# Two orders changed in a 4096 x 4096 matmul: quarter sums of A behind a sum of B, and the two units of one B block swapped

## The chip, the cores and the metric

The kernel runs on one core of a Trainium2 chip. The metric is the device time of one execution in microseconds (us). Before the change three runs gave 1533.63, 1534.99 and 1537.55 us, so the median is 1534.99 us.

## The reference

```python
def reference(a, b, alpha):            # a, b: 4096 x 4096 float32, alpha = 0.01
    x = np.matmul(a, b)
    return np.where(x > 0, x, alpha * x)
```

## The kernel before

**Tiling.** The output is cut into 4 row groups g and 4 column groups j of 1024 each; one pair (g, j) is a region. The first region, (0, 0), is computed plainly while the inputs arrive. The other fifteen follow in the order of the list `regions`: (0,1) (0,2) (0,3), then (1,2) (1,0) (1,3) (1,1), then (2,2) (2,0) (2,3) (2,1), then (3,2) (3,0) (3,1) (3,3). Within a region A is four blocks of 512 x 2048 (a11, a12, a21, a22) and B four blocks of 2048 x 512 (b11, b12, b21, b22), held in float16. Each block is two units of depth 1024, called k = 0 and k = 1; a unit of B is one tile of 128 x 4096 elements.

**Seven products instead of eight.** A region is made by a Winograd scheme: VectorE forms sums of A (s1, s2, s3, s4) and sums of B, TensorE runs seven products, and the results are added in PSUM or in SBUF. `PRODUCTS` (L653) lists the A operand and the place of the B operand of each. Product 0 is a11 by b11. The sums of B overwrite its blocks: at L1052 b12 becomes b12 - b22, at L1055 b11 becomes b11 + (b12 - b22), which product 2 takes (s2 by b11's place), and at L1116 b11's place becomes that sum minus b22, called t1 here, which product 4 takes (s1 by b11's place). A full product is 64 matmuls on each unit k, 128 columns of weights by 512 columns, into four PSUM banks.

**Quarters.** From row group 1 on, unless the next region begins a new row group, products 5 and 6 (the sixth and seventh) are themselves done by the same scheme in quarters: seven products of 16 matmuls with 256 columns. Their A operands are quarter sums of a22 and of s4 (`sums_of_a`, L693): four sums of 128 x 2048 elements, numbered 1 to 4, each stored to DRAM by SyncE (SP) as it is made (`kept_q`, L702), because every later region of the group loads them back (`load_sums`). Their B operands are quarter sums of b21 and b22 (`t3_of_b`, `sums_of_b`). In every region after the first of a group (g > 0) product 3 (the fourth) is done so too. `keep_x21` stores one more quarter of the block itself.

**Rooms.** `x_pool` has three rooms that are reused in turn. In the first region of a group they hold s2, s1 and s4; the next tile asked for, `t` at L1106, four quarters long, gets the room of s2 and can be written only when product 2 has read s2. `a16_pool` has three rooms of one quarter each; a room is free again when the store of what it held has landed. The eight DMA semaphores of SP and ScalarE are used in turn, so each issue also waits for the one eight before it.

**Order of work.** The schedule is written out by hand: each engine works through its instructions in program order. In a first region VectorE has, between products 1 and 4: the adds of product 1 (L973), the leaky step (L313), two sums for b21 (L1090), `keep_x21` and the four quarter sums of s4 (L1096, L1097), t1 in two sums (L1116, one for each k), the four quarter sums of a22 (L1121), then the quarter sums of b21 (L1161, L1162), the difference of b22 (L1163), `add_v` (L1164) and the adds of product 4 and of the quarter products (L973, L862). The quarter sums of s4 go to `new_a16`, and so do sums 1 to 3 of a22; the fourth goes to `t[:, 3]`, and the three quarter sums of b21 to `t[:, 0]`, `t[:, 1]`, `t[:, 2]`.

**B's loads.** `fetch_b` asks for the next region's blocks as soon as the products that read them have gone through: b12 behind product 3, b11 behind product 4 (L1184), b21 and b22 behind the quarter products. Most go through GpSimd's queue, half a unit (512 KB) at a time (L533). A second region's b11 is asked for by the first region with k = 0 ahead of k = 1, since `ks` there is (0, 1); in the second region itself `ks` is (1, 0), and product 0 reads k = 1 first:

```python
ks = (1, 0) if in_quarters else (0, 1)
todo = [(k, c) for k in ks for c in range(KC)]
```

The sums of B at L1052 and L1055 follow `ks` too: b12's unit 1, b11's unit 1, b12's unit 0, b11's unit 0, with the memset that releases the load of half of s2 between the first two (L1054).

Of the kernel before, what the change touches and what calls it, by code (L numbers as in the profile page):

```python
# [24 lines left out]
KC = 8  # L25
# [23 lines left out]
def kernel(  # L49
# [153 lines left out]
    def a_cols(t, c, mt, is_plain=False):  # L203
        rows = slice(mt * P, (mt + 1) * P)
        return plain(t)[:, c, rows] if is_plain else t[:, c // 2, rows, c % 2]
# [132 lines left out]
    order = [("b", 0), ("a", 0, 0, 1), ("a", 1, 0, 1), ("a", 2, 0, 1), ("a", 3, 0, 1)]  # L338
# [3 lines left out]
    for what, i, *more in order:  # L342
        if what == "a":
            r, tiles = more
            k = slice(r * rw, (r + 1) * rw)
# [106 lines left out]
    for i in range(1, len(steps)):  # L452
        t, h, u, first, last = steps[i]
# [19 lines left out]
        t, h, u, first, last = steps[i]  # L473
# [108 lines left out]
    def operand(g, name, k):  # L582
        if name[0] == "s":
            return s[g, name, k]
        return at[g, int(name[1]) - 1, 2 * (int(name[2]) - 1) + k]
# [90 lines left out]
    def quarters_of_a(g, name):  # L676
        return {(h, k): operand(g, name, k)[:, :, h * HALF:(h + 1) * HALF, :] for h in range(2) for k in range(2)}
# [15 lines left out]
    def sums_of_a(g, name, room):  # L693

        x = {key: q.rearrange("p c m e -> p c (m e)") for key, q in quarters_of_a(g, name).items()}
        made = {}

        def make(n, x0, x1, op):
            made[n] = room(n)
            f = lambda t: made[t].rearrange("p (c m) -> p c m", m=2 * HALF) if isinstance(t, int) else x[t]  # L700
            nc.vector.tensor_tensor(f(n), f(x0), f(x1), op)
            nc.sync.dma_start(kept_q[name][n - 1], made[n])  # L702

        make(1, (1, 0), (1, 1), ADD)
        make(2, 1, (0, 0), SUB)
        make(3, (0, 0), (1, 0), SUB)
        make(4, (0, 1), 2, SUB)

    def x21(g, name):
        return operand(g, name, 0)[:, :, HALF:, :]  # L710

    def by_chunk(t):
        return t.rearrange("p c m e -> p c (m e)") if len(t.shape) == 4 else t.rearrange("p (c m) -> p c m", m=2 * HALF)

    def keep_x21(g, name):
        if g < G - 1:
            nc.sync.dma_start(by_chunk(kept_x21[name]), by_chunk(x21(g, name)))
# [45 lines left out]
    def new_a16(_=None):  # L763
        return a16_pool.tile([P, QUARTER], DT, name="q16", tag="a16")
# [18 lines left out]
    for i, (g, j) in enumerate(regions):  # L783

        ks = (1, 0) if in_quarters else (0, 1)
# [11 lines left out]

        def product(n, banks, first):
            name, half, nt = PRODUCTS[n]
            todo = [(k, c) for k in ks for c in range(KC)]  # L800
            order = [(mt, k, c) for k, c in todo for mt in range(MT)]
            if n == 0 and late_s2:

                order = [(mt, k, c) for k in ks for mts in ((0, 1), (2, 3)) for c in range(KC) for mt in mts]
            for mt, k, c in order:
                t = operand(g, name, k)
                nc.tensor.matmul(  # L807
                    banks[mt], a_cols(t, c, mt, t is first_a), B(half, nt, k)[:, c, :],
                    start=first and (k, c) == todo[0], stop=(k, c) == todo[-1], skip_group_check=not first,
                )  # L810
# [188 lines left out]
        def fetch_a(h, half, n):  # L999
            if n == 0:  # L1000
                coming["rows", h, half] = small_pool.tile([P, 16], FP32, name="rows", tag=f"rows{half}")
            coming[h, half][n][0]()
# [21 lines left out]
        first_of_group = i == 0 or regions[i - 1][0] != g  # L1024
        in_quarters = g > 0 and not turning
        in_fourth = in_quarters and not first_of_group
        second_of_group = in_fourth and regions[i - 2][0] != g
# [3 lines left out]
        if first_of_group and g:  # L1031
            keep_s2(g)

        product(0, y, True)
        if second_of_group:
            sums_of_s3(g, (2,))
# [5 lines left out]
        if have_t2:  # L1042
            for k in ks:
                t = have_b[i, k, 0] = b_pool.tile([P, KC, NT], DT, name="b", tag="b11")
# [23 lines left out]
        bring_a(0, 0, range(3 if g else 4))  # L1068

        product(1, z, True)  # L1070
        add(u1, z)
        leave(u1_pairs, 0, 0)
# [18 lines left out]
        if turning and g:  # L1091
            t3_of_b(quarters_of_b(i, 0, 1))
            for n in range(3):
                fetch_a(0, 1, n)
        if first_of_group and g:
            keep_x21(g, "s4")  # L1096
            sums_of_a(g, "s4", new_a16)  # L1097
        if not g:
            bring_a(0, 1)

        product(2, y, False)
        if late_ones:
            late_ones[0].begin()
        u2_pairs, u2 = keep(y, 1 - side)
        if g:
            t = x_pool.tile([P, 4, QUARTER], DT, name="q", tag="x")  # L1106
# [10 lines left out]
        if late_ones:  # L1117
            late_ones[0].end()
        if in_quarters and first_of_group:
            sq = {4: t[:, 3]}  # L1120
            sums_of_a(g, "a22", lambda n: sq.setdefault(n, sq[4] if n == 4 else new_a16()))  # L1121
            keep_x21(g, "a22")
# [106 lines left out]
    with tc.If(even == 0):  # L1229
        for m in range(M // RM):  # L1230
            a_blocks = []
            for u in range(KU):
                t = a_pool.tile([P, KC // 2, RM, 2], BF16, name="a", tag=f"a{u // 2 + 1}{m % 2 + 1}")
# [6 lines left out]
            for n in range(N // NT):  # L1240
                banks = [new_bank(n % 2 * 4 + mt) for mt in range(MT)]
                cols = slice(n * NT, (n + 1) * NT)
                for u in range(KU):
                    t = b_pool.tile([P, KC, NT], BF16, name="b", tag=f"b{u // 2 + 1}{n % 2 + 1}")
# [8 lines left out]
                for mt in range(MT):  # L1253
                    t = c_pool.tile([P, 2, NT], FP32, name="c", tag=f"c{side}")[:, 0]
# [44 lines left out]
```

## Time and profile before

| what | value |
|---|---|
| median of three runs | 1534.99 us (1533.63 to 1537.55) |
| the profiled execution's own time | 1536.2 us |
| its span, first to last instruction | 1534.2 us |
| busy: TensorE / VectorE / ScalarE / GpSimd | 1524.3 / 1158.9 / 425.5 / 258.5 us |
| granted TensorE clock | 0.999 |
| HBM read and written, over the span | 300 GB/s |

The span is split by region as follows, by the first matmul of each in the timeline: (1,2) begins at 411.1 us, (1,0) at 505.2, (2,2) at 784.6, (2,0) at 878.1, (3,2) at 1157.6, (3,0) at 1251.7. A full product takes 13.8 us there, a product in quarters 12.2 us. In the table a busy time is the sum over the whole span; where an engine's queue stood still, and for whom, is in the views of waits and in the timeline.

### The profile page before, as it was taken

Reading aid. Unit: us, or ns where it says so; the run is one execution under the profiler, and the core shown is the slowest. Engines: PE = TensorE matmul, PEld = TensorE weight load, DVE = VectorE, ACT = ScalarE, POOL = GpSimd, SP = SyncE. Lnnn points to the kernel's source line nnn. Section 1 sums busy time; section 2 is a strip of 40 time slices with the busy share of each in tenths; the row PEclk is TensorE's granted clock in tenths of the full one; section 3 lists DMA queues with packets and bytes.
Section 4 is the critical chain, followed back from the end, with each engine's and each line's share of the span. In section 5 each row is a group of like instructions: output and inputs, shape, how many; then the busy total and the mean of one; then the engine's idle time right before and its main releaser. Section 6 shows DMA issues by size and latency. Waiting matters only on the chain. (4 is left out here: it accounts for less than half of the span.)

```text
span 1534.2 us, 21785 instructions
## 1 busy us (share of the span) xinstructions
PE 1524.3 (99%) x8667; PEld 847.1 (55%) x8667; DVE 1158.9 (76%) x1207; ACT 425.5 (28%) x730; POOL 258.5 (17%) x426
## 2 busy tenths in 40 slices
PE   9999999999999999999999999999999999999998
PEld 4444444444446567574544747557544475746656
DVE  4368867765699686768769698676976987687677
ACT  2201344646310213103641130312464103041210
POOL 5641110143202011022220001010331100101000
PEclk9999999999999999999999999999999999999999
DMA  9999995998879999899797939669899892948723
GB/s 246 186 215 203 237 281 169 180 197 172 231 277 287 258 278 275 251 289 255 170 288 266 321 148 208 260 157 322 166 241 283 235 349 72 294 162 190 301 97 140
DMA packets 192002, 351.26 MB, mean 229 GB/s; under 512 B 18705, under 2 KB 131601, under 8 KB 178834
## 3 DMA queue, kind: packets, MB, share of 16 engines
q0 software_dynamic: 119808, 112.22, 46.2%
q1 hardware_dynamic: 65458, 211.98, 37.0%
q10 hardware_dynamic: 6624, 25.56, 4.4%
q8 instruction: 70, 1.15, 0.3%
q14 instruction: 42, 0.34, 0.1%
HBM read 344.98 MB, written 114.82 MB: 300 GB/s over the span
## 5 line engine op out<-in xcount | busy, mean ns | idle before, releaser
L807 PE MATMUL ps<-b,a 128*128 128x512 f16 x2624 | 571.1, 379 | 0.5 <-DMA b<-in_b_dram 0.3
L807 PE MATMUL ps<-b,s 128*128 128x512 f16 x2240 | 489.2, 379 | 0.0
L807 PEld LDWEIGHTS <-a 128*128 128x128 f16 x2624 | 256.7, 98 | 308.8 <-issue 1.5
L807 PEld LDWEIGHTS <-s 128*128 128x128 f16 x2240 | 219.1, 98 | 262.5 <-issue 0.4
L589 DVE TENSOR_TENSOR b<-b 128x4096 f16<-128x4096 f16 x104 | 234.6, 2286 | 42.7 <-DMA b<-in_b_dram 34.1
L533 POOL DMA_DIRECT2D b<-in_b_dram x128 | 94.9, 746 | 860.1 <-PE ps L752 437.2
L820 ACT COPY c<-ps 128x512 f32<-128x512 f32 x164 | 84.8, 596 | 469.1 <-PE ps L807 433.3
L142 DVE STREAM_TRANSPOSE a<-a 128x512 uint32<-128x512 uint32 (+2 forms) x120 | 127.0, 1106 | 100.8 <-DMA a<-in_a_dram 100.8
L133 POOL DMA_DIRECT2D a<-in_a_dram x252 | 137.6, 554 | 266.8 <-ACT junk L608 98.2
L608 ACT ACTIVATE junk<-a 128x512 bf16<-128x512 f16 x192 | 121.1, 631 | 99.1 <-DMA a<-in_a_dram 93.8
L752 PEld LDWEIGHTS <-q 128*128 128x128 f16 x1424 | 139.3, 98 | 16.7 <-issue 0.6
L313 DVE SCALAR_TENSOR_TENSOR c<-c 128x1024 f32<-128x1024 f32 (+2 forms) x123 | 141.5, 1190 | 3.8 <-ACT c L820 3.5
L973 DVE TENSOR_TENSOR c<-ps,c 128x512 f32<-128x512 f32 x140 | 87.5, 682 | 55.5 <-PE ps L807 41.8
L231 ACT ACTIVATE sq<-b 128x2048 bf16<-128x2048 f16 x64 | 118.3, 1910 | 37.1 <-DVE sq L240 29.4
L752 PEld LDWEIGHTS <-a 128*128 128x128 f16 x1200 | 117.4, 98 | 18.0 <-issue 0.4
L283 PE MATMUL ps<-b,a 128*128 128x512 f16 x512 | 112.4, 379 | 0.6 <-DVE part L324 0.2
L752 PE MATMUL ps<-b,q 128*128 128x256 f16 x784 | 92.0, 273 | 0.4 <-DVE c L862 0.4
L752 PE MATMUL ps<-b,a 128*128 128x256 f16 x752 | 88.3, 273 | 0.0
L283 PEld LDWEIGHTS <-a 128*128 128x128 f16 x512 | 49.7, 98 | 61.2 <-issue 2.1
L909 ACT COPY c<-ps 128x512 f32<-128x512 f32 x9 | 5.3, 586 | 269.7 <-PE ps L752 148.3
L752 PEld LDWEIGHTS <-s 128*128 128x128 f16 x624 | 61.0, 98 | 7.1
L862 DVE TENSOR_TENSOR c<-ps,c 128x512 f32<-128x512 f32 x80 | 52.2, 683 | 14.4 <-PE ps L752 14.4
(104 smaller groups left out, 904.8 us busy)
## 6 DMA issues: line engine op xcount, KB each, us to landing
b<-in_b_dram POOLq DMA_DIRECT2D x136, 512.0 KB, 11.7
out_dram<-c SPq DMA_DIRECT2D x240, 256.0 KB, 6.3
a<-in_a_dram POOLq DMA_DIRECT2D x244, 128.0 KB, 5.8
b<-kept_half SPq DMA_DIRECT2D x28, 1024.0 KB, 10.9
b<-kept SPq DMA_DIRECT2D x20, 1024.0 KB, 9.2
q<-kept_qs ACTq DMA_DIRECT2D x40, 512.0 KB, 7.8
s<-kept_s SPq DMA_DIRECT2D x18, 1024.0 KB, 7.7
q<-kept_qa SPq DMA_DIRECT2D x28, 512.0 KB, 7.3
```

What stands on the lines that cost most here:

```text
L133: nc.gpsimd.dma_start(a16[32 * q:32 * q + 32], src.rearrange("(g i) w -> i g w", i=32))
L142: nc.vector.transpose(part.rearrange("p c m e -> p c (m e)").bitcast(U32) .rearrange("p c (g i) -> p g c i", i=32), src[:, :, i * n:(i + 1 ...
L231: nc.scalar.activation(to, self.parts[n], SQUARE)
L283: nc.tensor.matmul(ps, a_cols(at[0, h, u], c, mt, (h, u) == (0, 0)), bt[0, u, nt][:, c, :], start=first, stop=last,)
L313: nc.vector.scalar_tensor_tensor(t, t, alpha, t, op0=MULT, op1=MAX if alpha <= 1 else MIN)
L533: nc.gpsimd.dma_start(t[:, c:c + 4, :], b_rows(j, u, c, 4, nt, g > 0))
L589: nc.vector.tensor_tensor(f(to), f(x0), f(x1), op)
L608: nc.scalar.activation(junk, piece[:, q, :], SQUARE, accum_out=to[:, 4 * n + q:4 * n + q + 1])
L752: nc.tensor.matmul(to[m], xq[:, c // 2, rows, c % 2], yq[:, c, :], start=first and c == 0 and m < banks, stop=c == KC - 1, skip_group_chec ...
L807: nc.tensor.matmul(banks[mt], a_cols(t, c, mt, t is first_a), B(half, nt, k)[:, c, :], start=first and (k, c) == todo[0], stop=(k, c) == t ...
L820: nc.scalar.copy(kept[mt], banks[mt])
L973: nc.vector.tensor_add(to, bank, to)
```

## The change

Two edits. In the first region of a group (g > 0), `keep_x21` and the quarter sums of s4 move behind t1, and they are written to `t`, in the room of s2, instead of to `a16_pool`: sum 1 to `t[:, 3]`, sum 2 to `t[:, 0]`, sum 3 to `t[:, 2]`, sum 4 to `t[:, 1]`. In the second region of a group product 0 takes b11's unit 0 first and unit 1 second. The other products, and the sums of B, keep their order.

```diff
         def product(n, banks, first):
             name, half, nt = PRODUCTS[n]
-            todo = [(k, c) for k in ks for c in range(KC)]
+            ks_here = (0, 1) if n == 0 and second_of_group else ks
+            todo = [(k, c) for k in ks_here for c in range(KC)]
             order = [(mt, k, c) for k, c in todo for mt in range(MT)]
             if n == 0 and late_s2:
-                order = [(mt, k, c) for k in ks for mts in ((0, 1), (2, 3)) for c in range(KC) for mt in mts]
+                order = [(mt, k, c) for k in ks_here for mts in ((0, 1), (2, 3)) for c in range(KC) for mt in mts]
...
-        if first_of_group and g:
-            keep_x21(g, "s4")
-            sums_of_a(g, "s4", new_a16)
         if not g:
             bring_a(0, 1)
 
         product(2, y, False)
...
         for k in ks:
             b_sum(B(0, 0, k), B(1, 1, k), B(0, 0, k), SUB)
         if late_ones:
             late_ones[0].end()
         if in_quarters and first_of_group:
+            keep_x21(g, "s4")
+            sums_of_a(g, "s4", lambda n: t[:, {1: 3, 2: 0, 3: 2, 4: 1}[n]])
             sq = {4: t[:, 3]}
             sums_of_a(g, "a22", lambda n: sq.setdefault(n, sq[4] if n == 4 else new_a16()))
             keep_x21(g, "a22")
```

## The prediction

> **What bounds the kernel now.** First the page: its first line says how busy TensorE is, the rest of the span is all that any reordering can give.
>
> ```profile
> PE 1524.3 (99%) x8667; PEld 847.1 (55%) x8667; DVE 1158.9 (76%) x1207; ACT 425.5 (28%) x730; POOL 258.5 (17%) x426
> ```
>
> The span is 1534.2 us, so TensorE idles 9.9 us, start and tail included. A gain over 0.3% (4.6 us, about what a measurement of this kernel can tell from no change) would need half of that. Second, TensorE's waits in the stretch from 411 to 600 us, regions (1,2) and (1,0); columns: us in all, times, longest.
>
> ```profile
> PE ps L752 <- DVE c L862: 0.4, 1, 0.4
> PE ps L807 <- DMA b<-in_b_dram: 0.3, 1, 0.3
> ```
>
> Both lie where the change works. Third, the timeline around them, and around product 2 of (1,0); columns: start, us, engine and operation, in brackets the idle time before and who ended it.
>
> ```profile
> 489.46 0.70 PE L752 MATMUL ps<-b,q 128*128 128x256 f16 x5 [0.45 <-DVE c L862]
> ...
> 505.18 1.89 PE L807 MATMUL ps<-b,a 128*128 128x512 f16 x8
> ...
> 507.38 4.91 PE L807 MATMUL ps<-b,a 128*128 128x512 f16 x22 [0.31 <-DMA b<-in_b_dram]
> ...
> 528.25 2.29 DVE L589 TENSOR_TENSOR b<-b 128x4096 f16<-128x4096 f16 x1 [8.61 <-DMA b<-in_b_dram]
> 530.50 0.06 DVE L770 MEMSET s<- 128x1 f16 x1
> 530.63 2.29 DVE L589 TENSOR_TENSOR b<-b 128x4096 f16<-128x4096 f16 x1
> ...
> 533.27 9.01 PE L807 MATMUL ps<-b,s 128*128 128x512 f16 x41
> ```
>
> See three things. At 489.46 a quarter product was held by VectorE's adds. At 507.38 product 0 of (1,0) was held by a load: b11's unit 1, which it reads first, landed at 507.33, unit 0 had landed at 496.03. And at 533.27 product 2 starts without a wait, but its B operand was finished at 530.63 + 2.29 = 532.92, only 0.35 us earlier, behind b22's unit 1, which landed at 528.13. Matmul starts are 0.216 us apart (0.109 with 256 columns); by starts the first stall costs 0.720 - 0.109 = 0.61 us, the second 0.686 - 0.216 = 0.47 us.
>
> Fourth, VectorE in (1,2):
>
> ```profile
> 458.58 1.21 DVE L701 TENSOR_TENSOR q<-s 128x2048 f16<-128x2048 f16 x1
> 459.82 1.23 DVE L701 TENSOR_TENSOR q<-q,s 128x2048 f16<-128x2048 f16 x1
> 460.97 1.22 DVE L701 TENSOR_TENSOR q<-s 128x2048 f16<-128x2048 f16 x1
> 462.71 1.23 DVE L701 TENSOR_TENSOR q<-s,q 128x2048 f16<-128x2048 f16 x1 [0.52 <-DMA kept_qs<-q]
> 463.85 4.49 DVE L589 TENSOR_TENSOR b<-b 128x4096 f16<-128x4096 f16 x2
> 468.37 1.23 DVE L701 TENSOR_TENSOR q<-a,a 128x2048 f16<-128x2048 f16 x1
> 470.41 1.23 DVE L701 TENSOR_TENSOR q<-q,a 128x2048 f16<-128x2048 f16 x1 [0.81 <-DMA kept_qs<-q]
> 472.40 1.23 DVE L701 TENSOR_TENSOR q<-a 128x2048 f16<-128x2048 f16 x1 [0.76 <-DMA kept_qs<-q]
> ```
>
> Its only idle time between 421 and 500 us is for rooms whose stores have not landed: 2.09 us. The pair at 463.85 is t1: its unit 0 is done about 466.1, product 4 starts at 466.30. Fifth, the DMA engines by stretch (the last two numbers: share of the 16 engines, GB/s):
>
> ```profile
> 459.00:463.00 4.00, 4.00 (x20) 1.83 (x19) 3.44 (x4) 0.00 (x0) 1.49 (x2) 1.00 0.50 144
> 463.00:480.00 17.00, 17.00 (x81) 7.74 (x79) 15.32 (x12) 2.05 (x4) 2.96 (x4) 1.00 1.12 290
> 480.00:505.00 25.00, 24.55 (x225) 21.75 (x224) 21.13 (x25) 1.17 (x2) 5.92 (x8) 1.00 1.14 293
> 505.00:526.00 21.00, 20.69 (x99) 9.40 (x97) 12.66 (x18) 10.54 (x10) 1.48 (x2) 1.00 1.18 258
> 526.00:531.00 5.00, 5.00 (x25) 2.27 (x24) 2.67 (x3) 0.00 (x0) 0.00 (x0) 1.00 1.24 206
> ```
>
> From 463 to 531 they are full without a break; half a unit of b22 issued at 498.65 lands 27 us later. What is added to that backlog, or missed before it, moves b22.
>
> **The change part by part.** Per first region four sums of 1.22 us, four stores of 512 KB and, in groups 1 and 2, one store of a quarter move; nothing is added or removed.
>
> *Region (1,2), VectorE.* t1 starts at 458.58 (product 2 ended at 452.65, so no new wait) and is done at 463.1. The s4 sums follow until 467.8: s2's room is free since product 2. The a22 sums want 467.8, 469.0, 470.1 and 471.3; 1 to 3 find their rooms free now. New waits stand for `t`: the fourth for the store of s4's sum 1, b21's three sums (wanted at about 473.7, 474.9, 476.0) for those of sums 2, 3 and 4. The stores would be issued at 464.4, 465.5, 466.6 and 467.8. Three stores of s4 took 2.8, 7.2 and 8.1 us in the trace, those of a22 6.7 to 7.7 landing 2.0 apart. With 7.5 for the first and 2.0 between them they land at 471.9, 473.9, 475.9 and 477.9: waits of 0.6, 0, about 0.3 and about 0.8 us. VectorE thus has 2.09 - 1.7 = 0.4 us less idle time (ends: 2.8 us stores, 2.1 less; 10.2 us, the slowest a22 store of the third group, some 2 us more). Behind it queue `add_v` and the adds up to the one at 488.73 that TensorE waited for, with no gap from 480.60 on: the 0.61 us stall shrinks by 0.4, taken as 0.5 with the 2.0 spacing at its kinder end (0.61 gone; worst, 2 added).
>
> *Regions (2,2) and (3,2), VectorE.* Idle for stores there is 0.36 and 0.40 us; ahead of product 4's adds it idles 4.38 (853.24) and 1.97 us (1226.77). With a22's latencies of 6.7 to 8.2 us in (2,2) the new waits come to 0.1 us. In (3,2), 5.3 to 10.2 us, the last would be up to 2.2 late against 1.97 plus the 0.40 saved: no time on TensorE.
>
> *The queues.* SP's order stays the same: product 1's stores, the quarter of s4, its sums, a22's. No store of c waits behind them, the next are issued at 487.70. But the s4 stores are moved past GpSimd's first two loads of b12, issued at 459.86 and 460.60. Before, the first store ran while the DMA engines were half idle (share 0.50) and landed at 462.6, as the loads' packets began. Now it is issued at 464.4, into the full stretch: 512 KB more stand in the backlog. Price: stores of 256 KB with the queue to themselves land 0.64 us apart (548.12 to 550.06), so 1.29 us for 512 KB. Ends: 0 if the loads use the idle half, and four stores, 5.2 us, if none is made up. I take 1.3, since what is not full before 463 is full after. Every later landing up to 531 moves by it, b22's unit 1 to 529.4; b11's and b21's have room (b21's unit 0 at 524.8, wanted at 525.0).
>
> *Region (1,0).* Product 0 finds unit 0 there: 0.47 us gone, and unit 1 (507.3 + 1.3) is wanted only 6.9 us after the start. b11's unit 1 is now read until the end of product 0, so the sum at L1055 waits for that; in (1,0) and (2,0) it starts at 530.63 and 903.43, long after products that end at 519 and 892. In (3,0) it moves from 1261.26 to about 1265.5, behind it b12's and b11's unit 0 (4.5 us) and the measuring adds at 1270.22, which start about 1272.3; the adds of product 1 at 1278.85 come 0.2 late at most, and VectorE waits 2.84 us for TensorE at 1293.31. Product 2 at 1279.3 has its operand at 1267.8. Cost 0, hidden by product 1 (13.8 us). The memset and the load of s2 stand ahead of that sum and do not move.
>
> *The sum.* TensorE comes to product 2 of (1,0) 0.5 + 0.47 = 0.97 us earlier, at 532.3. Its operand is finished at 532.92 + 1.3 = 534.2 and it starts at 534.25: 0.98 us later than before. TensorE is full afterwards, so that remains: +1.0 us, span 1535.2, the profiled execution 1537.2. That execution stood 1.2 us above the median; on the median it is 1534.99 + 1.0, and I say 1535.9. Ends: backlog 0 gives 532.97 against 533.27, -0.3; a backlog of 2.0 gives +1.7.
>
> A rule that speaks against the change: GpSimd's two issues at 459.86 and 460.60 would now lie beside t1. In the trace the issue at 466.77 (0.74 us) ran inside t1's second sum (466.05 to 468.34) and took what all sixteen of this stretch take, 740 to 752 ns; the next came 1.43 us later, after that sum had ended. The Trainium skill, "SBUF — State Buffer", section "A bandwidth-pool intuition that's wrong (but worth ruling out)", says that descriptors GpSimd writes for its DMAs can be held until VectorE's operation ends. The first row does not bear it out for this shape, the second might. By that rule the time would be 1539.2 (worked out among the rivals), by the first row it stays 1535.9.
>
> **The rivals.**
> Gain stands: the backlog is made up before 528, and product 2 has its operand by 532.3. For it: loads without stores beside them land faster (838.70 and 842.47 in (2,2), issued at 833.43 and 834.17). Against it: no stretch below a share of 1.1 until 531. The bound is both stalls, -1.1: 1533.9; with the 0.5 us stall near 1171, behind a chain of loads of A, also gone, 1533.4.
>
> Stores hold VectorE in the first regions: at 10.2 us per store 2 us in (1,2), on top of the sum: +1 to +3, 1536 to 1538. For it: 10.2 occurs; against it: only behind four loads.
>
> Slower by over 0.3%: b22's unit 1 comes late by all four s4 stores, 4 x 1.29 = 5.2 us. Product 2 of (1,0) starts at 532.92 + 5.2 = 538.1, +4.9, 1539.9. It decides from a landing of 532.8 instead of 528.13. Against it: three of the four stores already ran in the full stretch.
>
> GpSimd held by t1: the two issues wait from 459.86 until 463.1, 3.2 us in which the engines idle; with the 1.0 above +4.2, 1539.2. Against it the issue at 466.77.
>
> Nothing to see: stalls and backlog as now, 0.
>
> **How the numbers follow.** Forecast 0.6; gain stands 0.2; stores hold VectorE 0.08; four stores late 0.05; GpSimd held 0.03; nothing 0.04. Faster by over 0.3%: 0.01, out of the gain's share, since 4.6 us are not there. Slower by over 0.3%: the 0.05, half of the 0.03, and 0.01 for sums of several, 0.07 rounded down. Within: 0.92. The range reaches from the gain's far end, 1533.4, to the end of held VectorE, 1538.0, and leaves out about 0.1; the forecast's own range is 1534.7 to 1536.7.
>
> **What would show it.** t1 at 458.6 in (1,2), no wait of the sums on rooms before the fourth of a22, the stall at 489.46 under 0.2, product 0 of (1,0) without a wait; b22's unit 1 landing near 529.4 and a wait of about 2 us ahead of product 2 of (1,0), named for VectorE. Wrong if that landing stays at 528.1 or comes after 531, if VectorE waits over 3 us for stores in (1,2), or if (2,0) or (3,0) show a wait at product 2 that is not there now (0.1 us at 905.87).

## The result and the profile after

The kernel before took 1534.96 us (median of 22 runs, 1532.74 to 1537.79), the changed kernel 1542.78 us (median of 22 runs, 1534.14 to 1547.50). The ratio is 1.0041, with a 95% interval of 1.0029 to 1.0054: slower by 0.41%, outside the predicted range of 1533.4 to 1538.0. The changed kernel's runs also spread over 13 us where those of the kernel before spread over 5; a likely reason is given below. Two runs of the experiments, one of e1 at 4187.71 us and one of e4 at 2444.05 us, stand far above the others of their kernels, and the times below leave them out.

The profiled execution of the changed kernel took 1547.45 us, near the upper end, with a span of 1545.5 us, 11.3 more than the span before. The same work is done, as the busy times on the page of the changed kernel show; the second line, a group's (busy and mean ns of one, then the idle time before it and what ended it), names what was waited for:

```profile
PE 1526.6 (99%) x8667; PEld 847.7 (55%) x8667; DVE 1159.6 (75%) x1207; ACT 425.5 (28%) x730; POOL 258.4 (17%) x426
...
L809 PE MATMUL ps<-b,a 128*128 128x512 f16 x2624 | 574.9, 381 | 8.6 <-DMA b<-in_b_dram 8.6
```

TensorE's waits in the changed kernel over the whole run (us in all, times, longest); the two stalls that the prediction listed for before are not among them, and three others are:

```profile
PE ps L809 <- DMA b<-in_b_dram: 8.6, 2, 5.8
PE ps L809 <- DVE b L589: 1.6, 1, 1.6
```

In the timeline of the changed kernel they stand one in each second region, at (1,0), (2,0) and (3,0) (start, us, engine and operation, in brackets the idle time before and its releaser):

```profile
504.70 27.36 PE L809 MATMUL ps<-b,a 128*128 128x512 f16 x126
533.70 2.53 PE L809 MATMUL ps<-b,s 128*128 128x512 f16 x11 [1.64 <-DVE b L589]
...
878.56 8.80 PE L809 MATMUL ps<-b,a 128*128 128x512 f16 x40
893.17 9.06 PE L809 MATMUL ps<-b,a 128*128 128x512 f16 x29 [5.81 <-DMA b<-in_b_dram]
...
1259.67 8.80 PE L809 MATMUL ps<-b,a 128*128 128x512 f16 x40
1271.26 6.04 PE L809 MATMUL ps<-b,a 128*128 128x512 f16 x21 [2.80 <-DMA b<-in_b_dram]
```

Product 0 and product 1 of (1,0) now run through from 504.70 without a wait, and product 2 waits 1.64 us for VectorE, as predicted. The wait that costs most is in product 0 of (2,0), 40 matmuls after its start: 32 on b11's unit 0 and 8 on the first half of its unit 1 (a full product is 64 matmuls in all, 32 on each unit; the section on the kernel before counts 64 on each, which is a slip; product 0 of a second region takes two of its four banks through a whole unit ahead of the other two, so the second half is wanted after 8 matmuls on the first). The load of the second half of unit 1 had not landed. (3,0) repeats it.

Starts of the same matmul in the two profiled executions show where the time went:

| milestone | before, us | after, us | difference |
|---|---|---|---|
| first of (1,2) | 411.05 | 410.75 | -0.30 |
| first of (1,0) | 505.18 | 504.70 | -0.48 |
| product 2 of (1,0) | 533.27 | 533.70 | +0.43 |
| first of (2,0) | 878.14 | 878.56 | +0.42 |
| first of (3,0) | 1251.67 | 1259.67 | +8.00 |
| end of the span | 1534.2 | 1545.5 | +11.3 |

So the part that the prediction summed, up to product 2 of (1,0), came out at +0.43 where it said +0.98 (at +0.73 if the 0.30 by which (1,2) began earlier is taken out). Then 7.6 us are lost between the start of (2,0) and that of (3,0), and 3.3 us after it. By starts of matmuls the three waits are 1.81, 5.97 and 2.96 us. Behind the second 13 matmuls and behind the third 7 started about 0.427 us apart instead of 0.216, which is 2.64 and 1.34 us more. That is 14.7 us; less the two stalls that went (0.61 and 0.47) it would be 13.6, against 11.3 of span. The rest are losses that the kernel before has and the changed one has not: gaps between matmul starts of 0.11 us at 905.6, 0.34 at 1106.9 and 0.60 from 1171.4 to 1172.6, together about 1.0, and a longer tail of the span, 6.80 us from the start of the last matmul against 5.83.

The granted clock falls with those slow matmuls. Windows of the changed kernel around the wait in (2,0) (busy us and instructions of TensorE, its weight loads, VectorE, ScalarE, GpSimd; granted clock; DMA share; GB/s):

```profile
880.00:894.00 14.00, 8.19 (x38) 3.51 (x36) 12.07 (x19) 10.92 (x7) 0.00 (x0) 0.92 1.07 361
894.00:900.00 6.00, 6.00 (x19) 2.27 (x18) 4.78 (x5) 4.50 (x4) 0.00 (x0) 0.62 0.31 120
```

In the six microseconds after the wait TensorE is busy throughout, at a clock of 0.62. The Trainium skill, "TensorE: Matmul & The Clock Gate", Part 1, says that after an idle window of about 3.4 us TensorE's clock is halved and that it takes about as long of work to come back, after a number of matmuls that varies with the phase of a free-running window. The runs agree with the halving and the variation; a wait of 2.96 us was already enough here.

Why that load was late is seen one region earlier. VectorE in (1,2) of the changed kernel, where the prediction expected waits for rooms:

```profile
453.34 8.90 DVE L589 TENSOR_TENSOR b<-b 128x4096 f16<-128x4096 f16 x4
462.14 1.23 DVE L701 TENSOR_TENSOR q<-s 128x2048 f16<-128x2048 f16 x1
463.41 1.23 DVE L701 TENSOR_TENSOR q<-q,s 128x2048 f16<-128x2048 f16 x1
...
470.35 1.22 DVE L701 TENSOR_TENSOR q<-a,q 128x2048 f16<-128x2048 f16 x1
471.49 1.22 DVE L681 TENSOR_TENSOR b<-b 128x2048 f16<-128x2048 f16 x1
472.74 1.23 DVE L687 TENSOR_TENSOR q<-b 128x2048 f16<-128x2048 f16 x1
```

There is no bracket on any of them: the sums run without a gap. VectorE is not what got worse. In (2,2) the same order leaves the DMA engines idle first and then sends them s4's and a22's stores together with GpSimd's loads. Windows of 826 to 842 us, the kernel before (second number from the end: DMA share):

```profile
826.00:834.00 8.00, 8.00 (x39) 3.60 (x37) 7.61 (x7) 1.67 (x4) 0.57 (x1) 1.00 0.74 288
834.00:842.00 8.00, 8.00 (x38) 3.63 (x37) 7.93 (x7) 2.05 (x4) 2.40 (x4) 1.00 0.99 152
```

and the changed kernel:

```profile
826.00:834.00 8.00, 8.00 (x38) 3.63 (x37) 8.00 (x5) 2.05 (x4) 0.15 (x1) 1.00 0.29 102
834.00:842.00 8.00, 8.00 (x38) 3.60 (x37) 7.93 (x8) 2.05 (x4) 2.58 (x4) 1.00 0.94 183
```

Before, the four stores of s4's sums were issued from 827.6 to 831.6 and had landed by 834.3; GpSimd's loads began at 833.4. After, they are issued from 834.3 to 837.8, behind the first load at 833.9, and land from 838.2 to 848.0. The share falls from 0.74 to 0.29 in the stretch that they left. What that does to GpSimd's queue is in the view of DMA queues (packets, MB, share of the 16 engines; q0 is GpSimd's, q1 SP's, q10 ScalarE's). From 826 to 862 us, before:

```profile
q0 software_dynamic: 3651, 3.64, 64.0%
q1 hardware_dynamic: 1899, 4.93, 36.8%
```

and after:

```profile
q1 hardware_dynamic: 2383, 5.54, 44.8%
q0 software_dynamic: 2562, 2.56, 44.0%
```

Of the 4.19 MB that the eight loads of b12 and b11 bring, GpSimd's queue had moved 3.64 MB by 862 us before, and 2.56 after: 1.08 MB less. At the 206 GB/s that this queue moved when it had the engines to itself (before, 854 to 858 us: 0.83 MB in 4 us) that is 5.2 us, the same as four stores at the prediction's 1.29 us. But it no longer has them to itself. From 862 to 874 us in the changed kernel:

```profile
q10 hardware_dynamic: 535, 1.93, 40.4%
q1 hardware_dynamic: 624, 1.44, 34.3%
q0 software_dynamic: 710, 0.70, 34.1%
```

ScalarE's loads of the quarter sums and SP's loads and stores have begun, and GpSimd's queue gets 0.70 MB in 12 us, 58 GB/s. From 842 to 852, beside SP's queue alone, it moved 708 packets to SP's 709, but 0.71 MB to 2.58. So the packets are dealt out nearly equally (with three queues 535, 624 and 710 of 1869, less evenly), and GpSimd's are the small ones, about 1 KB. The Trainium skill, "DMA: Bandwidth & Descriptors", section "Queues, rings and completion order", says that each DMA engine takes turns between the queues packet by packet; these counts agree, closely with two queues and roughly with three. How many queues are at work is not all of it. From 874 us on ScalarE's queue has next to nothing left, and GpSimd's shares with SP's alone. From 874 to 878 us in the changed kernel:

```profile
q1 hardware_dynamic: 173, 1.29, 79.5%
q0 software_dynamic: 174, 0.18, 26.0%
```

and from 880 to 884:

```profile
q0 software_dynamic: 409, 0.40, 59.2%
q1 hardware_dynamic: 402, 0.73, 54.8%
```

The counts are nearly equal both times. Beside SP's packets of 7.5 KB GpSimd's queue moved 45 GB/s, beside packets of 1.8 KB 100. So what it gets also goes by the size of the packets that stand beside its own.

The last half of b11's unit 1 lands at 893.1 us instead of 876.8: 5.2 us of backlog have become 16.3. Single executions lie some 5 us apart (the table below), so 16.3 is not exact, but it is well above 5.2.

### The profile page after: what moved, and what is told of

It reads as the page before. It is cut to its first block, busy times and chain, and to the rows that moved or that the text cites. A ratio compares the mean times of both kernels' runs of the same rounds, so it can differ in the third digit from the quotient of the medians.

```text
span 1545.5 us, 21789 instructions
## 1 busy us (share of the span) xinstructions
PE 1526.6 (99%) x8667; PEld 847.7 (55%) x8667; DVE 1159.6 (75%) x1207; ACT 425.5 (28%) x730; POOL 258.4 (17%) x426
## 4 chain that ended last, share of the span: by engine, by line
PE 60%; DMA 5%; DVE 0%; issue 0%; POOL 0%
PE ps L809 42%; PE ps L752 18%; DMA b<-in_b_dram 5%; DVE b L589 0%; DVE c L940 0%; POOL b L533 0%; DVE c L313 0%; DVE c L975 0%
## 5 line engine op out<-in xcount | busy, mean ns | idle before, releaser
L975 DVE TENSOR_TENSOR c<-ps,c 128x512 f32<-128x512 f32 x140 | 87.6, 684 | 52.6 <-PE ps L809 51.3
L283 PEld LDWEIGHTS <-a 128*128 128x128 f16 x512 | 49.7, 98 | 60.8 <-issue 1.4
```

The costliest lines, as they stand in the source:

```text
L283: nc.tensor.matmul(ps, a_cols(at[0, h, u], c, mt, (h, u) == (0, 0)), bt[0, u, nt][:, c, :], start=first, stop=last,)
L975: nc.vector.tensor_add(to, bank, to)
```

## The experiments

Each result stands beside runs of the kernel before on the same chip: 1534.63 us in the first comparison (e1 to e4), 1534.64 in the second (e3b, e6, e7). For every kernel this table gives group 2's loads in its profiled execution: GpSimd's first load of b12 issued in (2,2), the last half of b11's unit 1 landed, and the time between.

| kernel | issued | landed | between, us | waits for b11 in (2,0) |
|---|---|---|---|---|
| before | 833.4 | 876.8 | 43.4 | none |
| after | 833.9 | 893.1 | 59.2 | 5.97 |
| e1, moved sums only | 838.8 | 899.6 | 60.8 | 5.80 and 7.27 |
| e2, product 0's order only | 832.0 | 880.8 | 48.8 | none |
| e3, e2 and four stores more | 838.0 | 895.9 | 57.9 | 4.64 |
| e3b, e2 and two stores more | 833.7 | 884.9 | 51.2 | none |
| e4, stores early | 832.4 | 876.6 | 44.2 | none |
| e6, moved in group 1 only | 834.2 | 880.6 | 46.4 | none |
| e7, ScalarE's loads on SP | 834.2 | 885.5 | 51.3 | none |

The four with the stores of group 2 in their old place or earlier and none added (before, e2, e4, e6) lie between 43.4 and 48.8 us: 5 us is how far single executions go apart. The changed kernel's 59.2 is 10.4 us above the highest of them and 15.8 above the lowest.

**e1: the moved sums alone.** The changed kernel with product 0 in the old order.

```diff
-            ks_here = (0, 1) if n == 0 and second_of_group else ks
+            ks_here = ks
```

> The move of s4's quarter sums alone; product 0 of the second regions reads b11's unit 1 first, as before. If the late landing of b11's unit 1 is the cause (theory: the four moved stores run beside the loads of b12 and b11), TensorE needs that unit 6.9 us sooner than in the changed kernel: in (2,0) its wait grows from 5.8 to about 12 us, in (3,0) from 2.8 to about 9, in (1,0) to about 3, each followed by a slower clock: 1553 to 1562 us. If the swapped order of the units is the cause (rival), this kernel is as fast as before, 1534 to 1536 us, and waits for no load of b.

Measured: 1558.02 us (the middle of three runs, 1556.49 to 1562.07), ratio 1.0144 (1.0123 to 1.0164). TensorE's waits for loads of b, and the waits in product 0 of (2,0) in its timeline:

```profile
PE ps L809 <- DMA b<-in_b_dram: 21.5, 6, 6.9
```

```profile
889.26 3.57 PE L809 MATMUL ps<-b,a 128*128 128x512 f16 x8 [5.64 <-DMA b<-in_b_dram]
899.69 5.66 PE L809 MATMUL ps<-b,a 128*128 128x512 f16 x17 [6.85 <-DMA b<-in_b_dram]
```

Product 0 waits at the first half of unit 1 and again at the second, in all three groups. The move alone costs about 23 us, and the second edit gives back about 15 of them (1558.02 against 1542.78, of different comparisons), by wanting unit 1 only 32 matmuls (6.9 us) later. The loads are as late as in the changed kernel (60.8 us against 59.2).

**e2: product 0's order alone.** The kernel before with the second edit.

```diff
-            todo = [(k, c) for k in ks for c in range(KC)]
+            ks_here = (0, 1) if n == 0 and second_of_group else ks
+            todo = [(k, c) for k in ks_here for c in range(KC)]
```

(and `ks_here` in the line of `late_s2`.)

> The swapped units of b11 alone; s4's sums and stores where they were. Theory: no load comes late, and the 0.47 us wait in product 0 of (1,0) is gone: 1534 to 1536 us, no wait of TensorE for a load of b. Rival (the swap, by way of the sum at L1055 that now waits for the end of product 0): the slow-down of the changed kernel is here, 1540 us or more, with waits of product 2 on VectorE.

Measured: 1534.03 us over 10 runs, ratio 0.9997 (0.9988 to 1.0007). No wait for a load of b is left, and the cost of the move is absent. The 0.47 us are too small for this measurement, so it can't be told from the kernel before. The loss comes with the first edit only.

**e3 and e3b: more stores, nothing else moved.** e2's kernel, in which SP stores a22's quarter sums a second time, into a DRAM tile that nobody reads: all four (e3), or the first two (e3b). VectorE's order is that of before.

```diff
             nc.sync.dma_start(kept_q[name][n - 1], made[n])
+            if name == "a22" and n in (1, 2, 3, 4):
+                nc.sync.dma_start(scratch[n - 1], made[n])
```

> The swapped units, s4's sums where they were, and each of the four quarter sums of a22 stored twice, the second time to a place that nobody reads: 2 MB more beside the loads of b12 and b11, with VectorE's order untouched. Theory: b11's unit 1 lands in (2,0) some 10 to 16 us later than the 876.8 of before and TensorE waits for it there, 3 to 8 us: 1538 to 1548 us. Rival (VectorE's order, t1 ahead of s4, is the cause): no wait for loads of b, 1534 to 1536 us.

Measured: 1550.08 us (four runs, 1546.71 to 1555.22), ratio 1.0096 (1.0065 to 1.0127). Its waits for b:

```profile
PE ps L811 <- DMA b<-in_b_dram: 8.6, 2, 4.5
PE ps L811 <- DVE b L589: 3.5, 1, 3.5
```

Stores alone make the same waits at the same places, without t1 or the s4 sums changing place: one ahead of product 2 of (1,0), one in product 0 of (2,0) and one in that of (3,0). Its loads take 57.9 us, 9.1 to 14.5 us more than those of the four undisturbed kernels, for 2 MB that would be 5.2 us at the full rate.

> As the run with each quarter sum of a22 stored twice, but only sums 1 and 2: 1 MB more beside the loads instead of 2 MB. If the loads only queue behind the stores' bytes (1.29 us for each 512 KB), b11's unit 1 lands in (2,0) 2.6 us later than in the kernel with the swapped units alone (880.8), 883.4, before TensorE wants it: no wait there. If each byte left over is moved at a third of the rate, because other queues have come in, it lands 5 to 8 us later, 886 to 889, and TensorE waits up to 3 us: 1535 to 1540 us.

Measured: 1535.21 us, ratio 1.001 (0.9999 to 1.0021), unit 1 landing 4.1 us later than in e2, with loads issued 1.7 us later. The time between grew by 2.4 us, about the 2.6 of the full rate; but single executions go 5 us apart, so e3b does not decide at which rate one store more is paid. What it does show is a landing that was still in time: with two stores more, unit 1 landed at 884.9, no wait for a load of b appeared, and the time hardly moved.

**e4: the stores early, the sums late.** VectorE in the order of the changed kernel, but the four stores into `kept_q["s4"]` go out ahead of product 2, from parts of s1. It leaves out the stores of the true sums, so what later regions load is not s4's sums; only its time is of use.

```diff
+        if first_of_group and g:
+            for n in range(4):
+                part_s1 = s[g, "s1", n // 2].rearrange("p c m e -> p (c m e)")
+                nc.sync.dma_start(kept_q["s4"][n], part_s1[:, n % 2 * QUARTER:(n % 2 + 1) * QUARTER])
...
-            sums_of_a(g, "s4", lambda n: t[:, {1: 3, 2: 0, 3: 2, 4: 1}[n]])
+            sums_of_a(g, "s4", lambda n: t[:, {1: 3, 2: 0, 3: 2, 4: 1}[n]], False)
```

> The changed kernel with its order on VectorE, but the four stores of s4's sums go out ahead of product 2, where they stood before, from a part of s1 that is ready by then. So what later regions load as s4's quarter sums is not those sums: the true sums are made and not stored, which leaves VectorE's time as it is. Theory: b11's unit 1 lands in time again, no wait for loads of b, 1533 to 1536 us. Rival (VectorE's order): still 1540 us or more.

Measured: 1534.28 us (the middle of nine runs), ratio 0.9992 (0.9982 to 1.0002), and no wait for a load of b. The stores of group 2 were issued from 823.8 to 826.2 and had landed by 831.1. With the same order on VectorE and as many bytes stored, the loss is gone. With e3, which makes the loss without that order, this shows that it is the place of the stores beside the loads, and not the order of the sums.

**e6: the move in group 1 only.** The second edit everywhere, the first only where g is 1.

```diff
+        if first_of_group and g > 1:
+            keep_x21(g, "s4")
+            sums_of_a(g, "s4", new_a16)
...
+            if g == 1:
                 keep_x21(g, "s4")
                 sums_of_a(g, "s4", lambda n: t[:, {1: 3, 2: 0, 3: 2, 4: 1}[n]])
```

> The swapped units everywhere, the move of s4's sums in row group 1 alone. The prediction's sum for (1,2) and (1,0) stands by itself here: two stalls of together 1.1 us gone, product 2 of (1,0) about 1.8 us late. Theory (the loss is made in (2,0) and (3,0), where the prediction had put nothing): 1534.5 to 1536.5 us, a wait at product 2 of (1,0), none in (2,0) and (3,0). Rival (the loss is spread over all three groups alike): a third of it, 1537 to 1538 us.

Measured: 1535.99 us, ratio 1.0003 (0.9993 to 1.0014). TensorE's waits for b, and the timeline at product 2 of (1,0) and at product 0 of (2,0):

```profile
PE ps L809 <- DVE b L589: 1.7, 1, 1.7
```

```profile
534.09 6.20 PE L809 MATMUL ps<-b,s 128*128 128x512 f16 x28 [1.72 <-DVE b L589]
...
878.95 21.32 PE L809 MATMUL ps<-b,a 128*128 128x512 f16 x98
```

This is the kernel that the prediction's sum describes: a wait of about 2 us at product 2 of (1,0), and nothing behind it. Its time is 6.8 us below that of the changed kernel (of another comparison), which is what groups 2 and 3 cost. From the kernel before its time can't be told apart, so the sum's +1.0 us itself is seen in the trace only.

**e7: one queue fewer beside the loads.** The changed kernel, with the quarter sums of s4 loaded through SP's queue instead of ScalarE's.

```diff
-                load_sums("s4", next_s, (n,), nc.scalar)
+                load_sums("s4", next_s, (n,), nc.sync)
```

> The changed kernel, with s4's quarter sums for the seventh product loaded by way of SP's queue instead of ScalarE's: the same bytes, two DMA queues instead of three while b11's unit 1 is on its way. If a queue's share goes by the number of queues that have work, b11 gets 71 GB/s instead of 58 between 862 and 874 us (0.15 MB more) and its unit 1 lands in (2,0) 1 to 3 us ahead of 893.1: 1538 to 1542 us. If the share goes by bytes waiting, nothing changes: 1541 to 1546 us.

Measured: 1535.48 us, ratio 1.0003 (0.9992 to 1.0015). Unit 1 landed at 885.5 instead of 893.1, and no wait for a load of b is left. The queues of e7 from 862 to 874 us:

```profile
q1 hardware_dynamic: 1015, 2.65, 62.0%
q0 software_dynamic: 1017, 1.01, 49.5%
```

With two queues GpSimd's gets half of the packets, 1017 of 2032, and 84 GB/s, against 710 of 1869 and 58 GB/s with three. The direction was expected, the size was not: 7.6 us instead of 1 to 3, between single executions that can lie 5 us apart. That the loss is gone does not hang on one execution: the ten runs lie between 1534.98 and 1538.35 us. The edit also made two of SP's loads, of 1 MB each, later by 2.5 and 0.6 us (issued at 865.5 and 866.0 instead of 863.0 and 865.4), and changed the packets that stand beside GpSimd's. How much is due to each, and how much to the number of queues, is not separated.

## Why the prediction was wrong, step by step

**Its two small gains: right.** Both stalls are gone, at 489.46 and at the start of (1,0). The sum's terms give 1535.97, where 1535.9 was put down; this changes nothing below.

**Room waits in (1,2): wrong, without consequence.** It expected 1.7 us. There were none in (1,2); in (2,2) there were three, of 0.28, 0.83 and 0.87 us at 843.85, 845.90 and 848.00, where 0.1 was expected, and in (3,2) three of 2.08, 0.79 and 0.80. TensorE waited for none of them.

**Backlog in (1,2), product 2 of (1,0): right in kind, unsure in size.** Taken was 1.3 us of backlog, b22's unit 1 at 529.4 and a wait of about 2 us; it landed at 528.76 (528.13 before) and the wait was 1.81. e6 shows that sum alone, within the forecast's own range of 1534.7 to 1536.7. But the backlog did not move every load alike, as the step assumed: b11's unit 1, put at 507.3 + 1.3, landed at 510.3, 3.0 us later than before. It was in time only because the second edit wants its last half at about 513.3; in e1, without that edit, product 0 of (1,0) waits for it 1.29 and 3.28 us. And "TensorE is full afterwards" holds only nearly, by the 1 us of small gaps behind (2,0) in the kernel before, which are gone in the changed one.

**The step that failed: "Regions (2,2) and (3,2) ... no time on TensorE".** It examined VectorE's waits for rooms in these regions and stopped there. The price of a store moved past GpSimd's loads, which the step on the queues had worked out, was not applied to their loads, and what is due there is not b22 but b11. The list of what would show it wrong names a wait at product 2 of (2,0) or (3,0); the waits came in product 0. The profile before had the numbers for it: the stores in (2,2) had landed at 834.3, as the loads began, so all four were moved from a half-idle stretch into the loads. And unit 1 landed at 876.8 with product 0 starting at 878.1; with the new order it is wanted at about 887, so there were some 10 us to spare. Four stores at 1.29 us would have used half of them, so the prediction's own price, carried over to (2,2), would still have given no wait.

**So the price failed too.** The four stores cost 16.3 us at the last landing (10.4 to 15.8 by the times between issue and landing), not 5.2. 1.29 us per store is the price in a stretch that one queue has to itself. The 1.08 MB that were left over had to move while other queues were at work: at 58 GB/s beside SP's and ScalarE's (862 to 874 us), and at 49 GB/s beside SP's from there to 893.1 (0.94 MB). The row that would have shown it was in the profile before: between 862 and 870 us, beside the same two, GpSimd's queue moved 0.51 MB, 64 GB/s.

**A cost that was not in the sum: the clock.** The waits of 5.97 and 2.96 us each took another 2.64 and 1.34 us.

**The rivals.** "b22's unit 1 comes late by all four s4 stores ... 1539.9" had the sign and, in (2,2), the number of stores, but named another load in another region, and its price by the full rate. Its condition, all four missing the idle stretch, was doubted for (1,2), rightly, and holds for (2,2). GpSimd held by t1 did not appear: the issues of the loads beside VectorE's sums in (2,2) took 740 to 752 ns, as before, and in (1,2) the first load, issued at 459.6 beside t1, landed 5.2 us later, against 10.4 before.

**The spread of the runs.** The last landing decides between nothing and a wait: in e7 (885.5) and e3b (884.9) it came before about 887 and product 0 ran through, in the changed kernel's profiled execution it came at 893.1. With 5 us from one execution to another, a margin used up explains that some runs of the changed kernel take 1534 and others 1547. The granted clock that is on record for each of the 22 runs fits: 0.999 or 1.000 in the seven up to 1538.55 us, 0.996 in the six above 1545, so the long runs had slow matmuls and the short ones hardly any. But only one execution has a trace, so that a late landing of b11 made the difference is argued, not shown.

## What to carry to other kernels

When a store is moved past loads, look in every group that repeats the move, not only in the first, for the last load behind it and the time at which it is wanted. Price the bytes that fall behind by the rate that the queue has at the time they will move, in company, not by its rate alone. Two edits can belong together: here one gave back about 15 of the 23 us that the other cost, and without the costly one it bought nothing that could be measured.

## What was not expected of the hardware

- The rate of one queue depends on what moves beside it. GpSimd's queue, with packets of 1 KB, moved 206 GB/s alone and 58 beside two others (862 to 874 us). Beside SP's alone it moved 45, 71 and 100 GB/s as SP's packets had 7.5, 3.6 and 1.8 KB (874 to 878, 842 to 852 and 880 to 884 us), with near equal counts of packets each time.
- Moving the loads of s4's quarter sums, 40 of 512 KB in the whole run, from ScalarE's queue to SP's made the changed kernel faster by 7.3 us (1542.78 to 1535.48, in different comparisons).
- Matmuls ran at half rate (0.427 us instead of 0.216) behind all nine waits of 2.96 us and more in the traces of the changed kernel, e1 and e3, for 7 to 13 matmuls or 1.3 to 2.7 us each (behind the third wait of e3, 4.25 us, only after four at full rate), and behind none of the five between 1.28 and 1.89 us (the changed kernel, e1, e6, e7).
